# Experts of a two-layer trunk: TensorE's instructions in a written order, returns and gather beside the transposes, one pool of five banks

## The chip, the cores and the metric

The kernel runs on one core of a Trainium2 chip. The metric is the device time of one execution in microseconds. A smaller number is better. Engines are named as in the profile: PE is TensorE (PEld its weight loads), DVE is VectorE, ACT is ScalarE, POOL is GpSimd, and SP issues nearly all DMAs. PSUM, into which TensorE writes, has eight banks of 128 partitions x 512 fp32 values here; all eight are used by the experts.

## The reference

The whole program is a trunk of two layers over 256 latent and 256 context tokens of width 1024: modulation, three mixing branches (attention, a diagonal scan, a gated linear recurrence), and a mixture of experts. The change touches only the experts. Layer 0 sends context and latents through them, layer 1 the latents alone:

```python
def hier_moe(h, w_group, b_group, w_expert, b_expert, w_gate, w_up, w_down):
    ...
    top_p, top_i = lax.top_k(jax.nn.softmax(le_sel, axis=-1), TOP_K)
    wts = p_g[:, None] * top_p / jnp.sum(top_p, axis=-1, keepdims=True)
    ...
    def expert_block(args):
        xblk, e = args
        return (jax.nn.silu(xblk @ w_gate[e]) * (xblk @ w_up[e])) @ w_down[e]

    yb = lax.map(expert_block, (xb, blk_e)).reshape(cap, dm)
    out = jnp.zeros((n_tok + 1, dm), h.dtype).at[buf_tok].add(yb * buf_w[:, None].astype(h.dtype))
    return out[:n_tok]
...
            ctx = ctx_mid + g2c * hier_moe(hcf.reshape(-1, dm), *moe_par).reshape(ctx_mid.shape)
...
        x = x + g2 * hier_moe(hxf.reshape(-1, dm), *moe_par).reshape(x.shape)
```

There are 32 experts in a layer, each with `w_gate` and `w_up` of 1024 x 512 and `w_down` of 512 x 1024, in fp32.

## The kernel before

**Blocks.** Every expert gets 32 rows (`ROWS`) of each token set for the tokens that chose it; more would go through `overflow`, a loop that runs zero times on this data. One call of `expert_rows` works on a block of 128 rows. In layer 0 that is 2 experts x 2 sets (context and latents) x 32 rows, and there are 16 such blocks (`ng`). In layer 1 it is 4 experts x 32 rows, in 8 blocks.

**Steps of a block**, all in `expert_rows` but the gather:

- *gate* (tile `pg`) and *up* (`pu`): 32 matmuls each, with 32 columns of stationary data and 512 of moving data; four of them, one for each 32 rows of the block, use different columns of the array and stand next to each other in the code (the loop over `a`). Every fp32 matmul has two records in the trace.
- `hd`: silu by ACT, the product by DVE; then four *transposes* into `pt` and a copy by ACT to `hT` (also a tile `hd`).
- *down* (`py`, line 1689): two halves of 512 columns, 16 matmuls each, in groups of four as above. ACT scales a half to `wh`, DVE takes the remainder to `wl` (lines 1692 and 1695). `wh` and `wl` have one buffer each.
- *returns* (`pc`, line 1706): `wh` and `wl` of a half are spread back to tokens through the one-hot matrix `ot`: in layer 0 eight matmuls for a half, two (`wh`, `wl`) for each of four banks; the matmuls of the two token sets use different halves of the array's rows and stand in pairs in the code. DVE multiplies a bank by the gain (`cw`, line 1711, two buffers), POOL adds it to the residual (`Xctx`, `Xx`, line 1713).
- *gather* (`expert_gather`, tile `py`, line 1617): picks the next blocks' rows from `mh` by a one-hot matrix `oh`; in layer 0 one gather serves two blocks, with four banks of eight matmuls, and each bank is read out by four instructions, ACT and DVE in turn (lines 1629 and 1627, into `xT`). `expert_slots` (tile `pt`, line 1642) finds each row's weight and token with four short matmuls a block, read by DVE (`sl`).

**Banks.** `pg`, `pu` and `pt` have one bank each, pool `py` three (down and gather), pool `pc` two (returns).

**Order.** The program is written block after block: gate, up, transposes, down with its returns, then the next gather. The order on each engine is made by the framework's scheduler, which orders by its own timeline; each engine then runs its instructions in that order. The last block is written under a high priority.

**Weights.** `expert_chunk` takes weights as chunks of 128 x 2048 fp32 (1.05 MB), 12 for a block of layer 0 and 24 in layer 1, 192 in a layer. `prefetch` issues them on SP's queue (line 189) in the order of use, into a ring of 15 buffers in layer 0 (7 + 4 + 4) and 19 in layer 1 (11 + 4 + 4). A chunk can be issued when the matmuls that read the chunk 15 (19) places before it are done.

Of the kernel before, what the change touches and what calls it, by code (L numbers as in the profile page):

```python
# [18 lines left out]
NT = 4  # L19
# [107 lines left out]
class Trunk:  # L127
# [1409 lines left out]
    def moe(self, l, rs):  # L1537
# [8 lines left out]
        self.py = es.enter_context(tc.tile_pool(name=f"py{l}", bufs=3, space=PSUM))  # L1546
        self.pc = es.enter_context(tc.tile_pool(name=f"pc{l}", bufs=2, space=PSUM))
# [30 lines left out]
        def gather(q, OH):  # L1578

            w = na * ROWS  # L1580
            x = self.expert_gather(OH, nq)
            return [(x[:, :, a], self.expert_slots([OH[:, :, w * a:w * a + w]] * self.ns, m * q + na * a, aux)) for a in range(nq)]
# [6 lines left out]
        for _ in range(NXT[l] - PRE[l]):  # L1589
            self.prefetch(self.X[x0])  # L1590
        for p in range(ng):
            if p % nq == 0:
                cur = nxt
            W = [[self.expert_chunk() for a in range(na)] for _ in range(6)]
            if p < ng - 1:
                self.expert_rows(*cur[p % nq], na, self.ns, W)
            else:
                with tc.high_priority():
                    self.expert_rows(*cur[p % nq], na, self.ns, W, True)
            if p % nq == 0 and p + nq < ng:  # L1600
                nxt = gather(p // nq + 1, picked(p // nq + 1))
# [3 lines left out]
    def expert_gather(self, OH, nq, aff=None):  # L1605

        nc = self.nc
        nt = NT - self.mx0
        ns = 1 if aff else self.ns
        nt //= ns  # L1610
        xT = self.m2.tile([128, 8, nq, 128], FT, name="xT", bufs=2)
        for jj in range(0, 8, 4 // ns):
            xp = self.py.tile([128, 2, 256], FT, name="py").rearrange("p a (b n) -> p (a b) n", b=2)
            for u in range(4):
                j, s = jj + u // ns, u % ns
                for t in range(nt):
                    nc.tensor.matmul(xp[:, u, :], self.mh[:, nt * s + t, 128 * j:128 * j + 128], OH[:, nt * s + t, :],  # L1617
                                     start=t == 0 and u == 0, stop=t == nt - 1 and u == 3)
# [11 lines left out]
        return xT  # L1630

    def expert_slots(self, OHs, col, aux):

        nc = self.nc
        nt = NT - self.mx0
        ns, n = len(OHs), aux.shape[-1]
        nt //= ns
        w = 128 // ns
        ap = self.pg.tile([128, 512], FT, name="pt")
        for s, OH in enumerate(OHs):  # L1640
            for t in range(nt):
                nc.tensor.matmul(ap[w * s:w * s + w, 0:n], OH[:, nt * s + t, :], aux[:, nt * s + t, :], start=t == 0, stop=t == nt - 1)  # L1642
# [9 lines left out]
    def expert_rows(self, xT, sl, na, ns, W, last=False):  # L1652
# [10 lines left out]
        OT = self.ot  # L1663
        for t in range(nt // ns):
            V.tensor_scalar(OT[:, 128 * t:128 * t + 128], self.c["one1"], sl[:, 1:2], -128.0 * t, op0=OP.subtract, op1=OP.is_equal)
        P = []
        for n in range(2):
            q = pg.tile([128, 512], FT, name=f"p{'gu'[n]}")
            for hf in range(2):
                for k in range(4):  # L1670
                    for a in range(ng):
                        nc.tensor.matmul(q[ps_[a]], xT[:, 4 * hf + k, ps_[a]], part(W[2 * n + hf][a % na], k),  # L1672
# [4 lines left out]
        V.tensor_mul(hd, hd, P[1])  # L1677
        tp = pg.tile([128, 512], FT, name="pt").rearrange("p (j n) -> p j n", j=4)
        for j in range(4):
            nc.tensor.transpose(tp[:, j, :], hd[:, j * 128:(j + 1) * 128], self.ident)  # L1680
        hT = m2.tile([128, 512], FT, name="hd", bufs=1).rearrange("p (j n) -> p j n", j=4)
        S.copy(hT, tp)  # L1682
        for i, (c0, m) in enumerate(((0, 512), (512, 256), (768, 256)) if last else ((0, 512), (512, 512))):
# [3 lines left out]
            for k in range(4):  # L1687
                for a in range(ng):
                    nc.tensor.matmul(Y[ps_[a]], hT[:, k, ps_[a]], part(W[4 + n][a % na], k)[:, c1:c1 + m], start=k == 0, stop=k == 3)  # L1689
# [6 lines left out]
            cs = slice(c0, c0 + m)  # L1696
            nb = 512 // m
            nu = nt // ns
            for t in range(0, nu, nb):
                cps = [self.pc.tile([128, 512], FT, name="pc").rearrange("p (t n) -> p t n", t=nb) for _ in range(ns)]  # L1700
                for u in range(nb):
                    for y in (yh,) if whole else (yh, yl):
                        for s in range(ns):
                            r = slice(128 // ns * s, 128 // ns * (s + 1))
                            ot = OT[r, (t + u) * 128:(t + u + 1) * 128]
                            nc.tensor.matmul(cps[s][:, u], ot.bitcast(FT) if whole else ot, y[r],  # L1706
                                             start=(u == 0 if whole else y is yh), stop=(u == nb - 1 if whole else y is yl))
                for s in range(ns):
                    at = nu * s + t
                    w = m2.tile([128, 512], FT, name="cw").rearrange("p (t n) -> p t n", t=nb)  # L1710
                    V.tensor_mul(w, cps[s], self.g2[1 if x0 + at < 2 else 0][:, None, cs].to_broadcast([128, nb, m]))  # L1711
                    x = self.X2[(x0 + at) // 2 * 2][:, (x0 + at) % 2:(x0 + at) % 2 + nb, cs]
                    (V if nb > 1 and at + nb == nt else G).tensor_tensor(x, x, w, op=OP.add)  # L1713
            if last and nt == NT:
                for t in range(nt):
                    S.activation(cut(m2.tile([128, 512], FT, name="hd", bufs=1)), X[t][:, cs], AF.Square,
                                 accum_out=self.nsp[:, t, i:i + 1])

    def overflow(self, l, ov):
# [8 lines left out]
        with tc.If(n > 0), tc.For_i(0, n, 1) as i:  # L1728
# [54 lines left out]
            self.expert_rows(self.expert_gather(OH, 1, aff)[:, :, 0], sl, 1, 1, W)  # L1783
# [25 lines left out]
```

## Time and profile before

| | |
|---|---|
| median of 3 runs | 2107.39 us (2102.23 to 2111.22) |
| the profiled execution | 2102.93 us, span 2101.0 us |
| PE busy over the span | 1843.7 us (88%), 12480 records |
| DVE, ACT, POOL busy | 1036.6, 536.8, 503.2 us |
| HBM | 573.15 MB read, 292 GB/s over the span |
| granted TensorE clock, mean | 0.959 |

Times inside the execution are us from the start of the span. The stretches that matter: layer 0 before its experts up to 692, layer 0's experts from 692 to about 1243, the dense part of layer 1 to about 1640, layer 1's experts to the end. The rows below have the details. In the page's slices a digit stands for a fortieth of the span (52.5 us).

### The profile page before, as it was taken

The numbers are of one execution on the slowest core, as the hardware profiler recorded it, in microseconds if no ns is written. First come the engines' busy times: TensorE is split into PE (matmuls) and PEld (weight loads), VectorE is DVE, ScalarE is ACT, GpSimd is POOL, SyncE is SP. The second block draws the span as 40 slices with busy tenths as digits, with TensorE's granted clock in tenths as the row PEclk, the third lists the DMA queues.
The fourth block names the chain that finished last, engine by engine and source line by source line (L and its number), as shares of the span: only waits on it lengthen the run. The fifth ranks groups of instructions, "written<-read, shape, count | busy, mean of one in ns | idle before, by whom it ended". The sixth has DMA issues, their size and how long they took to land. (4 is left out here: it accounts for less than half of the span.)

```text
span 2101.0 us, 31835 instructions
## 1 busy us (share of the span) xinstructions
PE 1843.7 (88%) x12480; PEld 1113.4 (53%) x12480; DVE 1036.6 (49%) x2368; ACT 536.8 (26%) x1002; POOL 503.2 (24%) x473
## 2 busy tenths in 40 slices
PE   5889999999998999999999979989999776777776
PEld 2766776775787433433333239878888321222221
DVE  7858657979564233332333254958977310111111
ACT  3233533432333111110111034364444200000000
POOL 1632133405210032232313232215511000000000
PEclk8999999999998999999999989998999899999999
DMA  8576585557865798979888926646458999999998
GB/s 311 181 247 210 209 296 180 191 212 246 307 245 201 311 394 350 382 318 394 343 334 324 405 92 206 178 162 211 139 196 327 371 419 420 419 420 419 420 419 318
DMA packets 172048, 615.88 MB, mean 293 GB/s; under 512 B 24660, under 2 KB 90324, under 8 KB 108916
## 3 DMA queue, kind: packets, MB, share of 16 engines
q1 hardware_dynamic: 146084, 579.96, 71.6%
q10 hardware_dynamic: 25712, 33.56, 4.6%
q8 instruction: 100, 1.64, 0.3%
q14 instruction: 56, 0.46, 0.1%
q0 software_dynamic: 96, 0.26, 0.0%
HBM read 573.15 MB, written 40.58 MB: 292 GB/s over the span
## 5 line engine op out<-in xcount | busy, mean ns | idle before, releaser
L1672 PE MATMUL pg<-wst,xT 128*32 128x512 f32 x1536 | 252.7, 638 | 40.7 <-DMA wst<-mgate 38.6
L1672 PE MATMUL pu<-wst,xT 128*32 128x512 f32 x1536 | 233.1, 619 | 49.3 <-DMA wst<-mup 49.3
L367 DVE TENSOR_TENSOR wl<-wst,wh 128x512 fp32r<-128x512 f32 x240 | 192.9, 806 | 112.4 <-ACT wh L364 109.2
L1689 PE MATMUL py<-wst,hd 128*32 128x512 f32 (+1 forms) x1600 | 221.3, 578 | 21.7 <-ACT hd L1682 12.1
L364 ACT CAST wh<-wst 128x512 fp32r<-128x512 f32 x256 | 156.8, 618 | 281.3 <-PE acc L349 101.1
L1713 POOL TENSOR_TENSOR Xx<-Xx,cw 128x512 f32<-128x512 f32 x92 | 117.4, 1282 | 459.8 <-DVE cw L1711 459.8
L1677 DVE TENSOR_TENSOR hd<-hd,pu 128x512 f32<-128x512 f32 x24 | 16.5, 688 | 370.9 <-PE pu L1672 370.8
L1713 POOL TENSOR_TENSOR Xctx<-Xctx,cw 128x512 f32<-128x512 f32 x64 | 81.8, 1278 | 474.0 <-DVE cw L1711 473.9
L1711 DVE TENSOR_TENSOR cw<-pc,g 128x512 f32<-128x512 f32 x160 | 106.5, 687 | 152.2 <-PE pc L1706 148.0
L349 PE MATMUL acc<-hTh,wl 128*128 128x512 f32 (+1 forms) x480 | 168.1, 355 | 7.3 <-DVE wl L367 7.2
L347 PE MATMUL acc<-hTh,wh 128*128 128x512 f32 (+1 forms) x480 | 170.8, 356 | 1.3 <-ACT wh L364 1.3
L347 PE MATMUL acc<-wh,hTh 128*128 128x256 f32 x528 | 160.8, 309 | 11.5 <-ACT hTh L341 6.4
L348 PE MATMUL acc<-wl,hTh 128*128 128x256 f32 x528 | 161.2, 306 | 9.9 <-DVE wl L367 9.9
L348 PE MATMUL acc<-hTl,wh 128*128 128x512 f32 (+1 forms) x480 | 169.4, 353 | 0.0
L1672 PEld LDWEIGHTS pu<-wst,xT 128*32 128x32 f32 x1536 | 58.1, 113 | 196.9 <-issue 110.5
L349 PE MATMUL acc<-wh,hTl 128*128 128x256 f32 x528 | 160.1, 309 | 0.0
L1672 PEld LDWEIGHTS pg<-wst,xT 128*32 128x32 f32 x1536 | 55.7, 115 | 185.8 <-issue 112.5
L1689 PEld LDWEIGHTS py<-wst,hd 128*32 128x32 f32 x1600 | 58.7, 109 | 136.3 <-issue 91.6
L347 PEld LDWEIGHTS acc<-wh,hTh 128*128 128x128 f32 x528 | 112.2, 214 | 19.5 <-ACT hTh L341 7.0
L348 PEld LDWEIGHTS acc<-wl,hTh 128*128 128x128 f32 x528 | 113.5, 215 | 12.6 <-DVE wl L367 11.2
L1617 PEld LDWEIGHTS py<-oh,mh 128*128 128x128 f32 x768 | 96.2, 201 | 34.4 <-issue 29.6
L349 PEld LDWEIGHTS acc<-wh,hTl 128*128 128x128 f32 x528 | 111.9, 215 | 4.3 <-issue 3.0
(484 smaller groups left out, 3197.4 us busy)
## 6 DMA issues: line engine op xcount, KB each, us to landing
wst<-mgate SPq DMA_DIRECT2D x128, 1024.0 KB
wst<-mup SPq DMA_DIRECT2D x128, 1024.0 KB
wst<-mdown SPq DMA_DIRECT2D x122, 1024.0 KB
wst<-ada_w SPq DMA_DIRECT2D x48, 1024.0 KB
wst<-w_in SPq DMA_DIRECT2D x48, 1024.0 KB
wst<-w_o SPq DMA_DIRECT2D x8, 1024.0 KB
wst<-w_out SPq DMA_DIRECT2D x8, 1024.0 KB
dg<-stg ACTq DMA_DIRECT2D x15, 512.0 KB
```

The source lines that it names most:

```text
L347: nc.tensor.matmul(out, a[0], b[0], start=start, stop=False)
L348: nc.tensor.matmul(out, a[0], b[1], start=False, stop=False)
L349: nc.tensor.matmul(out, a[1], b[0], start=False, stop=stop)
L364: nc.scalar.copy(r(wh), s)
L367: e.tensor_sub(r(wl), s, r(wh).bitcast(FT))
L1617: nc.tensor.matmul(xp[:, u, :], self.mh[:, nt * s + t, 128 * j:128 * j + 128], OH[:, nt * s + t, :], start=t == 0 and u == 0, stop=t == nt ...
L1672: nc.tensor.matmul(q[ps_[a]], xT[:, 4 * hf + k, ps_[a]], part(W[2 * n + hf][a % na], k), start=hf == 0 and k == 0, stop=hf == 1 and k == 3)
L1677: V.tensor_mul(hd, hd, P[1])
L1689: nc.tensor.matmul(Y[ps_[a]], hT[:, k, ps_[a]], part(W[4 + n][a % na], k)[:, c1:c1 + m], start=k == 0, stop=k == 3)
L1711: V.tensor_mul(w, cps[s], self.g2[1 if x0 + at < 2 else 0][:, None, cs].to_broadcast([128, nb, m]))
L1713: (V if nb > 1 and at + nb == nt else G).tensor_tensor(x, x, w, op=OP.add)
```

## The change

`moe` makes one pool `py` of five banks in place of `py` (3) and `pc` (2). `self.pe` issues every matmul of a block behind the one before it in program order (`issue_after`), so that the scheduler no longer orders TensorE among the experts' matmuls; the other engines are still ordered by it. The returns of a half become a function, `expert_back`, which `expert_rows` hands back instead of running it; the next block runs the first half's returns between its up and its transposes (`before`), and behind its transposes the gather for a later block and the second half's returns (`behind`). A gather is cut in parts, so that each of the two blocks of layer 0 that share one runs half of it. The writes to `ot` move behind the returns that still read the old one. In the last block the first half's returns stand behind the second `down` piece.

```diff
-        self.py = es.enter_context(tc.tile_pool(name=f"py{l}", bufs=3, space=PSUM))
-        self.pc = es.enter_context(tc.tile_pool(name=f"pc{l}", bufs=2, space=PSUM))
+        self.py = es.enter_context(tc.tile_pool(name=f"py{l}", bufs=5, space=PSUM))
+        self.ordered, self.pe_last = False, None
...
+        back = ()
         for p in range(ng):
             if p % nq == 0:
                 cur = nxt
+                if p + nq < ng:
+                    OH = picked(p // nq + 1)
             W = [[self.expert_chunk() for a in range(na)] for _ in range(6)]
...
+            b = list(back)
+
+            def before():
+                if b:
+                    b.pop(0)()
+
+            def behind():
+                nonlocal nxt
+                if p // nq * nq + nq < ng:
+                    nxt = gather(p // nq + 1, OH, p % nq)
+                while b:
+                    b.pop(0)()
+            last = p == ng - 1
+            with self.in_order(), tc.high_priority() if last else nullcontext():
+                back = self.expert_rows(*cur[p % nq], na, self.ns, W, last, before, behind)
+                for f in back if last else ():
+                    f()
...
+    def pe(self, fn, *args, **kw):
+        if not self.ordered:
+            return fn(*args, **kw)
+        with nullcontext() if self.pe_last is None else self.tc.issue_after(self.pe_last):
+            i = fn(*args, **kw)
+        self.pe_last = i.ins
...
         V.tensor_mul(hd, hd, P[1])
+        before()
         tp = pg.tile([128, 512], FT, name="pt").rearrange("p (j n) -> p j n", j=4)
         for j in range(4):
-            nc.tensor.transpose(tp[:, j, :], hd[:, j * 128:(j + 1) * 128], self.ident)
+            self.pe(nc.tensor.transpose, tp[:, j, :], hd[:, j * 128:(j + 1) * 128], self.ident)
         hT = m2.tile([128, 512], FT, name="hd", bufs=1).rearrange("p (j n) -> p j n", j=4)
         S.copy(hT, tp)
+        behind()
+        OT = self.ot
+        for t in range(nt // ns):
+            V.tensor_scalar(OT[:, 128 * t:128 * t + 128], self.c["one1"], sl[:, 1:2], -128.0 * t, op0=OP.subtract, op1=OP.is_equal)
+        back = []
...
+            back.append(lambda c0=c0, m=m, yh=yh, yl=None if whole else yl, i=i: self.expert_back(c0, m, yh, yl, ns, last, i))
+            if not later or last and i:
+                back.pop(0)()
+        return back
...
+            cps = [self.py.tile([128, 2, 256], FT, name="py").rearrange("p a n -> p (a n)").rearrange("p (t n) -> p t n", t=nb) for _ in range(ns)]
```

TensorE in the middle of layer 0's experts before, from the transposes of a block on (the row of x4 at line 1680 is the transposes, `pg`/`pu`/`py<-wst` are gate, up and down, `pc` the returns; rows without a count are single matmuls):

```order
L1680 MATMUL pt<-cst_all,hd 128x128 x4
L1689 MATMUL py<-wst,hd 32x512 x17
L1706 MATMUL pc<-wh,ot 128x512 x2
L1689 MATMUL py<-wst,hd 32x512 x15
L1706 MATMUL pc<-wl,ot 128x512 x2
L1672 MATMUL pg<-wst,xT 32x512
L1706 MATMUL pc<-wh,ot 128x512
L1706 MATMUL pc<-wl,ot 128x512
L1706 MATMUL pc<-wh,ot 128x512
L1706 MATMUL pc<-wl,ot 128x512
L1672 MATMUL pg<-wst,xT 32x512 x15
```

The same engine and place now, a whole block (`py<-wh` and `py<-wl` are the returns, `py<-oh` the gather, `pt<-aux` the slots):

```order
L1635 MATMUL pg<-wst,xT 32x512 x32
L1635 MATMUL pu<-wst,xT 32x512 x32
L1635 MATMUL py<-wh,ot 128x512 x2
L1635 MATMUL py<-wl,ot 128x512 x2
L1635 MATMUL py<-wh,ot 128x512 x2
L1635 MATMUL py<-wl,ot 128x512 x2
L1635 MATMUL pt<-cst_all,hd 128x128 x4
L1635 MATMUL py<-oh,mh 128x128 x16
L1635 MATMUL pt<-aux,oh 64x33 x4
L1635 MATMUL py<-wh,ot 128x512 x2
L1635 MATMUL py<-wl,ot 128x512 x2
```

Two more returns rows and the 32 matmuls of down end the block, and the next begins. Gate, up and down are each in one piece, and the returns are in pairs throughout.

DVE in layer 0 before, from the product `hd` of one block to that of the next (`cw` are the returns' read-outs, two buffers that POOL empties; the next block in turn has the gather's):

```order
L1677 TENSOR_TENSOR hd<-hd,pu 128x512
L1695 SCALAR_TENSOR_TENSOR wl<-py,sl,wh 128x512
L1711 TENSOR_TENSOR cw<-pc,g_1_6567 128x512
L1711 TENSOR_TENSOR cw<-pc,g_0_6565 128x512
L1711 TENSOR_TENSOR cw<-pc,g_1_6567 128x512
L1695 SCALAR_TENSOR_TENSOR wl<-py,sl,wh 128x512
```

DVE now, the first part of a block, after the product `hd`:

```order
L1761 TENSOR_TENSOR cw<-py,g_1_6564 128x512
L1761 TENSOR_TENSOR cw<-py,g_0_6562 128x512
L1732 SCALAR_TENSOR_TENSOR wl<-py,sl,wh 128x512
L1761 TENSOR_TENSOR cw<-py,g_1_6564 128x512
L1761 TENSOR_TENSOR cw<-py,g_0_6562 128x512
L1659 TENSOR_SCALAR xT<-py,r_c_5800,mod_103 128x2x64 x2
```

The second half's `wl` stands between the first half's read-outs. What follows on DVE in a block whose gather part is the second of a gather (in the other blocks the row of `oh` is missing):

```order
L1679 COPY sl<-pt 32x1 x4
L1659 TENSOR_SCALAR xT<-py,r_c_5800,mod_103 128x2x64
L1680 COPY sl<-pt 128x1
L1568 TENSOR_TENSOR oh<-cst_moe,code_6457 128x128 x4
L1761 TENSOR_TENSOR cw<-py,g_1_6564 128x512
L1761 TENSOR_TENSOR cw<-py,g_0_6562 128x512
L1718 TENSOR_SCALAR ot<-cst_moe,sl 128x128
L1659 TENSOR_SCALAR xT<-py,r_c_5800,mod_103 128x2x64
```

The last read-out of the gather's second bank (`xT`, last row) stands behind two read-outs of the returns, a write of `ot` and, in every second block, four of `oh`.

## Rows read from the trace of the kernel before

**Rows 1.** The page's second part: GB/s moved by DMA in 40 slices.

```profile
GB/s 311 181 247 210 209 296 180 191 212 246 307 245 201 311 394 350 382 318 394 343 334 324 405 92 206 178 162 211 139 196 327 371 419 420 419 420 419 420 419 318
```

**Rows 2.** Busy time by stretch: PE, PEld, DVE, ACT, POOL, then clock, DMA share, GB/s.

```profile
1000.00:1060.00 60.00, 56.85 (x424) 18.27 (x423) 18.60 (x40) 6.72 (x12) 15.42 (x13) 1.00 0.88 352
1980.00:2040.00 60.00, 44.20 (x232) 14.07 (x228) 7.48 (x18) 4.39 (x8) 4.99 (x4) 0.89 1.01 420
```

**Rows 3.** Chain of work that ended last: start, us, what.

```profile
1667.17 19.90 DMA wst<-mgate
...
2089.59 3.64 PE py L1689 x52
```

**Rows 4.** PE's timeline, layer 0's experts: start, us, instructions [idle before <-releaser]; whole cycle.

```profile
692.22 8.65 PE L1672 MATMUL pg<-wst,xT 128*32 128x512 f32 x64 [2.13 <-ACTq L1728]
...
1022.32 0.66 PE L1680 MATMUL pt<-cst_all,hd 128*128 128x128 f32 x4 [0.85 <-DVE hd L1677]
1023.65 4.48 PE L1689 MATMUL py<-wst,hd 128*32 128x512 f32 x34 [0.68 <-ACT hd L1682]
...
1094.55 0.66 PE L1680 MATMUL pt<-cst_all,hd 128*128 128x128 f32 x4 [0.85 <-DVE hd L1677]
...
1237.03 0.51 PE L1706 MATMUL pc<-wh,ot 64*128 64x512 f32 x2
```

**Rows 5.** PE's timeline, two places where blocks of one kind stand whole.

```profile
700.68 7.05 PE L1672 MATMUL pu<-wst,xT 128*32 128x512 f32 x64
707.55 4.47 PE L1672 MATMUL pg<-wst,xT 128*32 128x512 f32 x36
...
774.20 7.07 PE L1689 MATMUL py<-wst,hd 128*32 128x512 f32 x64
781.20 0.49 PE L1617 MATMUL py<-oh,mh 128*128 128x128 f32 x2
```

**Rows 6.** PE's timeline, a mixed stretch of layer 0.

```profile
986.59 0.43 PE L1642 MATMUL pt<-aux,oh 128*64 128x33 f32 x8
986.95 1.04 PE L1689 MATMUL py<-wst,hd 128*32 128x512 f32 x2
987.93 2.05 PE L1617 MATMUL py<-oh,mh 128*128 128x128 f32 x16
989.91 0.51 PE L1706 MATMUL pc<-wh,ot 64*128 64x512 f32 x2
990.25 0.40 PE L1706 MATMUL pc<-wl,ot 64*128 64x512 f32 x2
990.57 1.38 PE L1617 MATMUL py<-oh,mh 128*128 128x128 f32 x10
```

**Rows 7.** Groups by form, 690 to 1250: busy us, mean ns | idle before <-releasers.

```profile
L1711 DVE TENSOR_TENSOR cw<-pc,g 128x512 f32<-128x512 f32 x128 | 85.2, 687 | 133.2 <-PE pc L1706 129.1 <-POOL Xctx L1713 4.1
L1713 POOL TENSOR_TENSOR Xctx<-Xctx,cw 128x512 f32<-128x512 f32 x64 | 81.8, 1278 | 474.0 <-DVE cw L1711 473.9
L1629 ACT ACTIVATE xT<-py,mod,r_c 128x128 f32<-128x128 f32 x58 | 26.3, 457 | 88.3 <-PE py L1617 60.5 <-DVE xT L1627 27.4
L1627 DVE TENSOR_SCALAR xT<-py,r_c,mod 128x128 f32<-128x128 f32 x59 | 24.0, 407 | 21.6 <-ACT xT L1629 21.3
L1695 DVE SCALAR_TENSOR_TENSOR wl<-py,sl,wh 128x512 fp32r<-128x512 f32 x31 | 23.1, 746 | 92.1 <-ACT wh L1692 92.1
L1665 DVE TENSOR_SCALAR ot<-cst_moe,sl 128x128 fp32r<-128x128 f32 x32 | 21.3, 670 | 0.0
L1692 ACT ACTIVATE wh<-py,sl 128x512 fp32r<-128x512 f32 x31 | 21.3, 688 | 164.2 <-PE py L1689 82.1 <-PE pc L1706 82.1
L1677 DVE TENSOR_TENSOR hd<-hd,pu 128x512 f32<-128x512 f32 x16 | 11.0, 688 | 109.7 <-PE pu L1672 109.6
L1648 DVE COPY sl<-pt 32x1 f32<-32x1 f32 x60 | 9.2, 153 | 18.7 <-PE pt L1642 18.1
L1568 DVE TENSOR_TENSOR oh<-cst_moe,code 128x128 f32<-128x128 f32 x28 | 8.6, 362 | 0.6 <-PE py L1617 0.6
```

More of the change, by code (lines that the diff above doesn't have):

```diff
@@ L1 @@
 import math
-from contextlib import ExitStack
+from contextlib import ExitStack, contextmanager, nullcontext
 import numpy as np
@@ L1577, in moe, with gather @@
         self.ot = self.m2.tile([128, nt * 128], FR, name="ot", bufs=1)
-        def gather(q, OH):
+        def gather(q, OH, part=None):
             w = na * ROWS
-            x = self.expert_gather(OH, nq)
-            return [(x[:, :, a], self.expert_slots([OH[:, :, w * a:w * a + w]] * self.ns, m * q + na * a, aux)) for a in range(nq)]
+            if not part:
+                self.gx, self.gs = self.m2.tile([128, 8, nq, 128], FT, name="xT", bufs=2), []
+            self.expert_gather(OH, self.gx, None if part is None else slice(2 * part, 2 * part + 2))
+            for a in range(nq) if part is None else (part,):
+                self.gs.append(self.expert_slots([OH[:, :, w * a:w * a + w]] * self.ns, m * q + na * a, aux))
+            return [(self.gx[:, :, a], s) for a, s in enumerate(self.gs)]
         if l == 0:
@@ L1593, in moe, with in_order, expert_gather @@
                 cur = nxt
+                if p + nq < ng:
+                    OH = picked(p // nq + 1)
             W = [[self.expert_chunk() for a in range(na)] for _ in range(6)]
[L1595 to L1601, printed above, removed]
+            b = list(back)
[13 more added lines that the diff above has]
+                    f()
         es.close()
         self.mes.close()
-    def expert_gather(self, OH, nq, aff=None):
+    @contextmanager
+    def in_order(self):
+        self.ordered = True
+        yield
+        self.ordered = False
+    def pe(self, fn, *args, **kw):
[4 more added lines that the diff above has]
+        self.pe_last = i.ins
+    def expert_gather(self, OH, xT, js=None, aff=None):
         nc = self.nc
@@ L1610, in expert_gather @@
         nt //= ns
-        xT = self.m2.tile([128, 8, nq, 128], FT, name="xT", bufs=2)
-        for jj in range(0, 8, 4 // ns):
+        for jj in range(0, 8, 4 // ns)[js or slice(None)]:
             xp = self.py.tile([128, 2, 256], FT, name="py").rearrange("p a (b n) -> p (a b) n", b=2)
@@ L1650, in expert_slots, with expert_rows @@
         return sl
-    def expert_rows(self, xT, sl, na, ns, W, last=False):
+    def expert_rows(self, xT, sl, na, ns, W, last=False, before=lambda: None, behind=lambda: None, later=True):
         nc = self.nc
@@ L1671, in expert_rows @@
                     for a in range(ng):
-                        nc.tensor.matmul(q[ps_[a]], xT[:, 4 * hf + k, ps_[a]], part(W[2 * n + hf][a % na], k),
+                        self.pe(nc.tensor.matmul, q[ps_[a]], xT[:, 4 * hf + k, ps_[a]], part(W[2 * n + hf][a % na], k),
                                          start=hf == 0 and k == 0, stop=hf == 1 and k == 3)
@@ L1688, in expert_rows @@
                 for a in range(ng):
-                    nc.tensor.matmul(Y[ps_[a]], hT[:, k, ps_[a]], part(W[4 + n][a % na], k)[:, c1:c1 + m], start=k == 0, stop=k == 3)
+                    self.pe(nc.tensor.matmul, Y[ps_[a]], hT[:, k, ps_[a]], part(W[4 + n][a % na], k)[:, c1:c1 + m], start=k == 0, stop=k == 3)
             whole = last and m < 512
@@ L1695, in expert_rows @@
                 V.scalar_tensor_tensor(yl, Y, sl[:, 0:1], yh.bitcast(FT), op0=OP.mult, op1=OP.subtract)
[L1696 to L1717, printed above, removed]
+            back.append(lambda c0=c0, m=m, yh=yh, yl=None if whole else yl, i=i: self.expert_back(c0, m, yh, yl, ns, last, i))
+            if not later or last and i:
+                back.pop(0)()
+        return back
+    def expert_back(self, c0, m, yh, yl, ns, last, i):
+        nc = self.nc
+        V, G, S = nc.vector, nc.gpsimd, nc.scalar
+        x0, m2, X, OT = self.mx0, self.m2, self.X, self.ot
+        nt = NT - x0
+        cut = lambda t: t[:, 0:m]
+        whole = yl is None
+        cs = slice(c0, c0 + m)
+        nb = 512 // m
+        nu = nt // ns
+        for t in range(0, nu, nb):
+            cps = [self.py.tile([128, 2, 256], FT, name="py").rearrange("p a n -> p (a n)").rearrange("p (t n) -> p t n", t=nb) for _ in range(ns)]
+            for u in range(nb):
+                for y in (yh,) if whole else (yh, yl):
+                    for s in range(ns):
+                        r = slice(128 // ns * s, 128 // ns * (s + 1))
+                        ot = OT[r, (t + u) * 128:(t + u + 1) * 128]
+                        self.pe(nc.tensor.matmul, cps[s][:, u], ot.bitcast(FT) if whole else ot, y[r],
+                                         start=(u == 0 if whole else y is yh), stop=(u == nb - 1 if whole else y is yl))
+            for s in range(ns):
+                at = nu * s + t
+                w = m2.tile([128, 512], FT, name="cw").rearrange("p (t n) -> p t n", t=nb)
+                V.tensor_mul(w, cps[s], self.g2[1 if x0 + at < 2 else 0][:, None, cs].to_broadcast([128, nb, m]))
+                x = self.X2[(x0 + at) // 2 * 2][:, (x0 + at) % 2:(x0 + at) % 2 + nb, cs]
+                (V if nb > 1 and at + nb == nt else G).tensor_tensor(x, x, w, op=OP.add)
+        if last and nt == NT:
+            for t in range(nt):
+                S.activation(cut(m2.tile([128, 512], FT, name="hd", bufs=1)), X[t][:, cs], AF.Square,
+                             accum_out=self.nsp[:, t, i:i + 1])
```

12 lines of the change are left out of this document (5 added, 7 removed).

## The prediction

> **What bounds the kernel now.** I read the slices first, to part the program into stages. In layer 1's experts, the last nine slices, DMA moves 419 GB/s without a break; in layer 0's experts, from slice 14 on, it moves 311 to 405 [rows 1]. The busy times by stretch say the same of a stretch of 60 us of each: layer 1 has a DMA share of 1.01 and PE 44.2 of 60 us, layer 0 has 0.88 and PE 56.9 [rows 2]. The chain that ended last is a line of DMA steps through layer 1, 19.90 us for the eight chunks of one gate [rows 3], so a chunk costs 2.49 us wherever DMA is the bound, and nothing that TensorE does there moves the end. The place to look is layer 0's experts, from 692.22 to the end of the last down at 1237.03, which is 544.8 us [rows 4].
>
> There a cycle of two blocks lasts 72.2 us, from the transposes at 1022.32 to those at 1094.55 [rows 4]. Its 24 chunks would take DMA 59.7. So TensorE's queue sets the pace. Yet its work is less: a whole gate, up or down takes 6.87 us (700.68 to 707.55, and 7.00 to an instruction of another kind, so 0.13 for the switch) [rows 5]; a gather bank 1.98, a block's slots 0.36, a pair of returns 0.34 or 0.32 [rows 6]; the transposes some 0.6 [rows 4]. A block is 3 x 6.87 + 2 x 1.98 + 0.36 + 16 returns in eight pairs, 2.7, + 0.6 = 28.2, two are 56.4. Waits for `hd` and `hT` are 2 x (0.85 + 0.68) = 3.1 [rows 4]. The other 12.7 us are the price of mixing: one matmul of down alone holds the engine for 0.98 us (986.95 to 987.93) [rows 6], where in a whole piece its share is 6.87 / 32 = 0.21. High busy time hides this.
>
> **The change, part by part: TensorE.** The new order has no broken groups and seven switches a block. With a gather a block is gate 6.87, up 7.00, returns 1.4, transposes 0.6, gather 3.95, slots 0.36, returns 1.4, down 6.87: 28.5 us. The wait for the product `hd`, 0.85, lies behind the first returns (1.4), and the copy to `hT` behind the gather; both cost nothing as long as these have their banks.
>
> **What is late next: banks.** The five banks of `py` turn in the order of their use, and a block takes twelve: four returns, two gather, four returns, two down. So the gather's first bank is the one that the second half of the previous down holds, and the first half of down takes the gather's second. The trace of before has no such turn, so I lay it out from its durations [rows 7], with 0 at the end of up and 0.05 for a signal.
>
> - `hd` is done at 0.85; PE has the first returns until 1.35 and the transposes until 1.95. DVE reads out two return banks until 2.25 (0.69 each). `wh` has one buffer, so ACT writes the second half's `wh` only when the first returns have read the old one, 1.2 to 1.9, and DVE its `wl` from 2.25 to 3.0. Only then is the bank free: the gather starts at 3.05, a **wait of 1.1**.
> - The gather runs to 6.95, the slots to 7.3, the second returns to 8.7. The other two `cw` wait for POOL, 1.28 an addition with two buffers, until 4.9, in time.
> - A bank of the gather is read by ACT, DVE, ACT, DVE, each waiting for the one before (27.4 and 21.3 us of idle time name each other [rows 7]), 0.46 and 0.41. For the second bank DVE has in its queue, from 7.4 on: four `sl` (0.6), `xT` to 8.45, one `sl`, two `cw` to 10.0, `ot` (0.67) to 10.65, and the last `xT` to 11.05. Down starts at 11.1 and could at 8.7: a **wait of 2.4**. In six blocks four `oh` stand there too, 4 x 0.36 = 1.45 more.
>
> So a block lasts 11.1 + 3 x 6.87 = 31.7. That is above DMA's 12 x 2.49 = 29.9, and the ring of 15 keeps ahead.
>
> **The sum.** First block, with no returns and a slower first gate (692.22 to 700.68): 8.46 + 7.05 + 0.85 + 0.6 + 3.95 + 0.36 + 6.87 = 28.1. Thirteen blocks of 31.7: 412.1. `oh` in six: 8.7. The last two have no gather; their second returns wait for `wl` until 3.05, and down for the fourth `cw` until 4.95, so 4.95 + 20.6 = 25.6 each, 51.1. In the last the first returns stand between the pieces of down: 1.4. Together 501.4, which is 43.4 less than 544.8.
>
> Layer 1's experts stay with DMA. Only the end is touched: the last chain step on PE [rows 3] holds both short pieces of down, and now four returns, 4 x 0.33, stand between them where before they fell into the waits for chunks: +1.3, bounds 0 and 1.5. The dense part of layer 1 has the same instructions, some in another place on PE, since the scheduler's timeline moved: 0, and as no row prices it I allow 6 either way. It waits on the experts' end, so the gain passes on.
>
> The profiled execution took 2102.9 (span 2101.0), so 2102.9 - 43.4 + 1.3 = 2060.8. The median of the runs is 4.5 above that execution; the range covers this.
>
> [...] Rows 5 price a switch between whole pieces at 0.13. [...]
>
> **Rivals.**
>
> *No bank waits, DMA sets the end.* If read-outs are quicker than laid out (`ot` is dearest, and only a mean), a block falls to 28.5, below DMA's 29.9. From the start 177 chunks are left to load, 441 us, and with the first and the last half piece, 3.4 each, the stage lasts some 450: 2009, or 2009 to 2040 where part of the waits goes. Against it: the one buffer of `wh` and `wl` and DVE's order are facts of the program.
>
> *The waits take all.* DVE and POOL are asked for the same work in bursts, `cw` behind POOL, `xT` behind `cw`. If the waits double, 3.5 more in 14 blocks or 49 us, the time is that of before, 2086 to 2112. For it: DVE waited for POOL already, 4.1 us [rows 7]; against it: POOL needs 8 x 1.28 = 10.2 of 31.7.
>
> *The clock.* In layer 1, where PE waits for every chunk, the granted clock falls to a mean of 0.89; in layer 0 it is 1.00 [rows 2]. If the new waits bring layer 0 to 0.89, each block's 28.5 us of work grow by 3.5, 56 in 16 blocks: 2117, slower than before. It decides from a loss of 2.7 a block, a mean clock below 0.91. Against it: two waits in 32 us, where layer 1 has one every 2.5, and the waits of 0.85 and 0.68 on both sides of the transposes left 1.00. [...]
>
> *TensorE was full.* If its 95% busy in layer 0 were all work, the order could bring nothing: 2103 to 2107. The 0.98 us for one matmul speaks against it, and the new order of the program does show whole pieces.
>
> **How the numbers follow.** The forecast, 2040 to 2086, has 0.67; no bank waits 0.15; waits that take all 0.10; the clock 0.06; TensorE full 0.02. One in ten lies below 2028 and one in ten above 2090: of the first rival a third is in the range, of the second little. A measurement of this kernel can tell about 0.5% from no change, 10.5 us. Faster by more: 0.67 + 0.15 + 0.05 of the second rival = 0.87; within: 0.07; slower: 0.06. The likeliest case gives 2061.
>
> **What would show it.** In the profile after: whole pieces of 6.87 us for gate, up and down in layer 0, and no single matmul of 0.98; a cycle of two blocks of some 64.9 instead of 72.2; PE idle for about 1.1 before the gather and 2.4 or 3.8 before down, with DVE as the releaser (`wl`, then `xT`); 380 to 400 GB/s; the stage some 43 us shorter; and layer 1's DMA steps still 19.9. Wrong would be: no idle before down, a granted clock under 1.00 in layer 0, or a dense part of layer 1 that differs by more than 6 us.

## The result, and the profile after

The changed kernel takes **2025.97 us** (median of 4 runs, 2022.45 to 2029.73) against 2106.44 of the kernel before (4 runs beside them, 2102.23 to 2111.22): ratio 0.9618, 95% interval 0.959 to 0.9645. The forecast was 2061 with a range of 2040 to 2086, and one chance in ten was put below 2028: the sign and the place were right, but the time lies under the range, and the gain was 80 us where 42 to 46 were expected. The profiled execution took 2025.23, span 2023.5.

DMA's line on the page, which answers to [rows 1]: slices 15 to 22 (counted from 1), layer 0's experts, now stand at 418 to 419 GB/s like layer 1's; before, the same slices stood at 318 to 394.

```profile
GB/s 323 164 236 257 142 353 193 171 167 255 239 365 113 251 418 418 419 418 419 418 419 418 359 103 244 131 201 191 102 250 366 419 420 419 420 420 419 420 420 293
```

Busy time by stretch (columns as in [rows 2]), first layer 0's experts in the kernel before, from the first gate to about the end of the last down:

```profile
692.22:1236.40 544.18, 526.72 (x3966) 195.75 (x3969) 169.04 (x353) 66.85 (x120) 151.44 (x121) 1.00 0.87 349
```

and the same stage in the kernel after, with the stretch of 60 us of [rows 2]:

```profile
694.19:1156.75 462.56, 441.90 (x3978) 186.05 (x3978) 171.01 (x357) 67.32 (x123) 152.05 (x122) 0.99 1.00 411
...
1000.00:1060.00 60.00, 57.43 (x525) 25.97 (x524) 24.15 (x51) 9.01 (x17) 22.13 (x18) 1.00 1.01 419
```

The stage is 82 us shorter, and PE's busy time fell by 85 with the same work; its idle time (first number less second) rose from 17.5 to 20.7. So the whole gain of the stage is time that the engine counted as busy and that was no work, and DMA's share went from 0.87 to 1.00.

PE's timeline of one block after, from its transposes to those of the next (columns as in [rows 4]):

```profile
968.81 0.66 PE L1635 MATMUL pt<-cst_all,hd 128*128 128x128 f32 x4
969.30 3.81 PE L1635 MATMUL py<-oh,mh 128*128 128x128 f32 x32
...
973.40 0.50 PE L1635 MATMUL py<-wh,ot 64*128 64x512 f32 x2
...
976.31 7.07 PE L1635 MATMUL py<-wst,hd 128*32 128x512 f32 x64 [1.69 <-DVE cw L1761]
983.20 7.05 PE L1635 MATMUL pg<-wst,xT 128*32 128x512 f32 x64
990.07 7.05 PE L1635 MATMUL pu<-wst,xT 128*32 128x512 f32 x64
997.05 0.50 PE L1635 MATMUL py<-wh,ot 64*128 64x512 f32 x2
...
998.17 0.66 PE L1635 MATMUL pt<-cst_all,hd 128*128 128x128 f32 x4
```

The pieces are whole, 6.87 us each; the block lasts 29.36, its neighbour (no `oh`) 28.55, the pair 57.9 us where 64.9 were forecast and DMA's 24 chunks take 59.7. There is no wait before the gather. The only wait left stands before down, 1.69 here and 0.87 in the neighbour, and its releaser is a read-out `cw`, not `xT`. DVE's timeline of the same block shows why this speaks against the prediction:

```profile
969.73 0.74 DVE L1732 SCALAR_TENSOR_TENSOR wl<-py,sl,wh 128x512 fp32r<-128x512 f32 x1
...
975.57 1.28 DVE L1761 TENSOR_TENSOR cw<-py,g 128x512 f32<-128x512 f32 x2
976.77 0.93 DVE L1718 TENSOR_SCALAR ot<-cst_moe,sl 128x128 fp32r<-128x128 f32 x1
977.62 0.40 DVE L1659 TENSOR_SCALAR xT<-py,r_c,mod 128x128 f32<-128x128 f32 x1
```

The gather began at 969.30, before `wl` had begun to read the bank of the last down half: it has another bank. Down began at 976.31, behind the first of the two `cw` at 975.57 and 1.3 us before the gather's last `xT`: it has a bank of the returns. The banks do not turn in the order of their use.

The end, which answers to [rows 3], in the chain after:

```profile
2000.31 8.59 DMA wst<-mdown
...
2008.95 7.56 PE py L1635 x66
```

From the last landing to the end of the span it is now 14.55 us, before 11.41.

### The profile page after: what moved, and what is told of

Its sections match the earlier page's. It is cut to its first block, busy times and chain, and to the rows that moved or that the text cites. A ratio compares the mean times of both kernels' runs of the same rounds, so it can differ in the third digit from the quotient of the medians.

```text
span 2023.5 us, 31822 instructions
## 1 busy us (share of the span) xinstructions
PE 1751.5 (87%) x12480; PEld 1102.0 (54%) x12480; DVE 1035.3 (51%) x2368; ACT 535.3 (26%) x1002; POOL 501.8 (25%) x473
## 5 line engine op out<-in xcount | busy, mean ns | idle before, releaser
L1635 PE MATMUL pu<-wst,xT 128*32 128x512 f32 x1536 | 220.6, 631 | 52.7 <-DMA wst<-mup 52.6
L1635 PE MATMUL pg<-wst,xT 128*32 128x512 f32 x1536 | 220.5, 640 | 49.5 <-DMA wst<-mgate 48.1
L1635 PE MATMUL py<-wst,hd 128*32 128x512 f32 (+1 forms) x1600 | 194.1, 594 | 41.7 <-DMA wst<-mdown 24.1
L347 PE MATMUL acc<-hTh,wh 128*128 128x512 f32 (+1 forms) x480 | 171.1, 357 | 1.5 <-ACT wh L364 1.5
L347 PE MATMUL acc<-wh,hTh 128*128 128x256 f32 x528 | 161.2, 310 | 10.6 <-ACT hTh L341 6.4
L1635 PEld LDWEIGHTS py<-wst,hd 128*32 128x32 f32 x1600 | 53.3, 113 | 169.0 <-issue 104.4
L1729 ACT ACTIVATE wh<-py,sl 128x512 fp32r<-128x512 f32 (+1 forms) x50 | 33.5, 670 | 369.2 <-PE py L1635 367.1
L347 PEld LDWEIGHTS acc<-wh,hTh 128*128 128x128 f32 x528 | 112.7, 216 | 17.0 <-ACT hTh L341 7.1
L1761 DVE TENSOR_TENSOR cw<-py,g 128x512 f32<-128x512 f32 x160 | 105.3, 685 | 27.1 <-PE py L1635 13.5
```

What stands on the lines that cost most here:

```text
L347: nc.tensor.matmul(out, a[0], b[0], start=start, stop=False)
L1635: i = fn(*args, **kw)
L1729: S.activation(yh, Y, AF.Identity, scale=sl[:, 0:1])
```

## The experiments

All times beside are of profiled executions. Every experiment but e8 and e10 was run once; single runs of the kernel before lie between 2094.8 and 2111.2, so a time that differs by less than some 10 us proves nothing by itself, and the timelines decide. "Stage" is from the first gate of layer 0's experts to the first matmul of the next dense part (L347 in the timelines); busy, idle and clock are of that stage without its last 21.5 us. What lies behind the last down is really 16.9 to 22.0 us in these runs, so busy time is up to 4.6 us too small (most in e5; 3.8 in e1 and e2); idle time is not touched by this. "Rounds" is counted from the order of PE's instructions, in layer 0's 16 blocks: in each stretch of weight matmuls between two instructions of another kind, the number of matmuls in the fullest of the four column tiles. With whole groups of four it is 384, and 6.87 / 8 = 0.86 us is one round.

| kernel | time | stage | PE busy | idle | clock | rounds |
|---|---|---|---|---|---|---|
| before | 2102.9 | 565.7 | 526.7 | 17.5 | 1.00 | 433 |
| after | 2025.2 | 484.1 | 441.9 | 20.7 | 0.99 | 384 |
| pool alone (e1) | 2057.8 | 514.8 | 465.7 | 27.6 | 1.00 | 402 |
| after, banks 3 + 2 (e2) | 2075.6 | 535.2 | 471.0 | 42.7 | 0.96 | 384 |
| after, order free (e3) | 2062.6 | 523.7 | 484.8 | 17.4 | 1.00 | 416 |
| after, banks in strict turn (e4) | 2073.6 | 534.8 | 457.4 | 55.9 | 0.96 | 384 |
| before's order, fixed (e5) | 2087.4 | 549.6 | 453.9 | 74.2 | 0.99 | 384 |
| returns in up, in groups (e6_mid) | 2076.2 | 533.1 | 464.7 | 46.9 | 0.99 | 399 |
| returns in up, between groups (e6_edge) | 2050.0 | 503.6 | 457.9 | 24.2 | 0.98 | 384 |
| returns in up, at steps (e9) | 2106.3 | 561.2 | 491.9 | 47.8 | 0.99 | 429 |
| half the returns (e7) | 2025.8 | 485.5 | 435.5 | 28.5 | 0.99 | 384 |

**Banks in strict turn** (e4). The step of the prediction in doubt, made true: five tiles of one buffer, taken by a counter.

```diff
+    def bank(self):
+        self.bn += 1
+        return self.py.tile([128, 2, 256], FT, name=f"py{'abcde'[self.bn % 5]}")
-            xp = self.py.tile([128, 2, 256], FT, name="py").rearrange("p a (b n) -> p (a b) n", b=2)
+            xp = self.bank().rearrange("p a (b n) -> p (a b) n", b=2)
```

(and so for `Y` and `cps`.) Expected:

> The changed kernel, in which the five banks for gather, returns and down are five tiles of one buffer each, taken in strict turn in the order of their use; all else is unchanged. Theory A (the prediction's reading of banks was right for a strict turn, and the changed kernel simply doesn't turn its banks): TensorE waits about 1.1 us before the gather for wl and 2.4 (3.8 with oh) before down for the last xT, two blocks take 63 to 66 us instead of 57.9, layer 0's experts some 500 us instead of 462.5, the time is about 2064. Theory B (the banks do turn, and my durations for the read-outs were too long): nothing changes, 57.9 and 462 us, 2026.

Its PE timeline, the two waits of a block and the one before down in its neighbour:

```profile
943.90 5.34 PE L1639 MATMUL pyd<-wst,hd 128*32 128x512 f32 x32 [3.36 <-issue]
949.02 3.64 PE L1639 MATMUL pye<-wst,hd 128*32 128x512 f32 x32
...
969.17 2.05 PE L1639 MATMUL pye<-oh,mh 128*128 128x128 f32 x16 [1.06 <-DVE wl L1736]
...
977.04 3.64 PE L1639 MATMUL pya<-wst,hd 128*32 128x512 f32 x32 [2.55 <-issue]
```

The layout of the prediction stands in it to a tenth: 1.06 before the gather (1.1), 2.55 before down (2.4), 3.36 with `oh` (3.85). The last `xT`, which down waits for there, reads `pya`, the bank that down then takes. The page puts down's wait to "issue", but DVE's timeline of this kernel has the last `xT` from 976.54 to 976.94, and down begins at 977.04. Even so the stage is 51 us longer than after's, not 38. By the table 35 of them are idle time and 15 busy time, and these are the clock: the first half of down at 943.90 takes 5.12 us where the second takes 3.44, and ten of the 16 blocks have such a slow first half (1.7 us longer each, one 2.7). The granted clock by stretch says so:

```profile
940.00:944.00 4.00, 0.64 (x10) 0.24 (x10) 3.97 (x12) 0.46 (x1) 1.87 (x2) 1.00 1.02 422
944.00:949.00 5.00, 5.00 (x32) 1.61 (x35) 1.91 (x3) 0.00 (x0) 3.14 (x3) 0.66 0.59 244
949.00:952.00 3.00, 3.00 (x32) 1.10 (x28) 0.75 (x1) 0.69 (x1) 0.00 (x0) 1.00 0.62 177
```

Theory A, with a part missing: the clock.

**Each half of the change alone** (e1 to e3). The pool alone, in the kernel before:

```diff
-        self.py = es.enter_context(tc.tile_pool(name=f"py{l}", bufs=3, space=PSUM))
-        self.pc = es.enter_context(tc.tile_pool(name=f"pc{l}", bufs=2, space=PSUM))
+        self.py = es.enter_context(tc.tile_pool(name=f"py{l}", bufs=5, space=PSUM))
```

(`cps` then comes from `py`.) Banks 3 + 2 is its mirror, the new order on the old pools:

```diff
-        self.py = es.enter_context(tc.tile_pool(name=f"py{l}", bufs=5, space=PSUM))
+        self.py = es.enter_context(tc.tile_pool(name=f"py{l}", bufs=3, space=PSUM))
+        self.pc = es.enter_context(tc.tile_pool(name=f"pc{l}", bufs=2, space=PSUM))
```

(`cps` comes from `pc` again.)

The free order is the kernel after with one line changed:

```diff
-        self.ordered = True
+        self.ordered = False
```

Expected:

> The kernel before with the one pool of five banks alone. Theory A (banks are not what it waits for, broken groups are): within 10 us of the kernel before, the stage 535 to 550 us. Theory B (the pool gives a good part of the gain): the stage at or below 520, 2080 or less.

> The changed kernel with the banks of before: three for gather and down, two for the returns. Theory A (the one pool is needed by the new order): the third and fourth bank of four returns wait for the read-outs of the first two, 1.5 us twice a block, so two blocks take 61 to 64 us in place of 57.9, the stage 480 to 500 in place of 462.5, the time 2043 to 2065. Theory B (the order alone matters): 57.9, 462.5, 2026.

> The changed kernel without the fixed order: the program's text stands as changed (returns and gather beside the transposes, one pool), but TensorE's instructions are placed by the scheduler's own estimate. It breaks about three groups of four in a block and puts the gather elsewhere than behind the transposes. Theory A (the fixed order carries the gain): a block costs 3 x 0.77 us for the broken groups and 1.5 for the waits for hd and hT more, two blocks take 64 to 66 us, the stage 510 to 525, the time 2075 to 2090. Theory B (the new places in the text carry it): 57.9 and 462.5 us, 2026.

My theory A for the pool fell: alone it shortens the stage by 51 us. In PE's timeline of that kernel the weights stand in far fewer stretches (63 in the stage; before 112, after 17), the returns in fours, and a broken group is left here and there:

```profile
954.72 0.66 PE L1679 MATMUL pt<-cst_all,hd 128*128 128x128 f32 x4 [0.90 <-DVE hd L1676]
956.05 1.05 PE L1688 MATMUL py<-wst,hd 128*32 128x512 f32 x2 [0.67 <-ACT hd L1681]
957.02 0.43 PE L1641 MATMUL pt<-aux,oh 128*64 128x33 f32 x8
957.39 3.63 PE L1688 MATMUL py<-wst,hd 128*32 128x512 f32 x30
...
1018.95 0.66 PE L1679 MATMUL pt<-cst_all,hd 128*128 128x128 f32 x4 [0.91 <-DVE hd L1676]
```

The cycle of two blocks is 64.2 (954.72 to 1018.95), before 72.2. The scheduler, with two banks for the returns, placed other work between single returns; with five it places them together. So part of the mixing came from the pools, which I had read only as a wait. The order alone (banks 3 + 2) gives 30 us, and its waits are the expected ones, for the read-outs of two banks:

```profile
PE pc L1636 <- DVE cw L1762: 39.0, 35, 2.2
```

Its time, 2075.6, lies above theory A's upper end (2065), again with a clock of 0.96. The free order keeps 42 of the 82 us: as theory A has it, the fixed order carries the other 40, though the total is better than its 2075. 51 and 30 add up to the whole, 82, though DMA may hold the whole down (e7 below).

**Whole pieces with nothing in the waits** (e5): the pool of five and the chain of the kernel after, on the text of the kernel before. The edit passes each matmul and transpose of the old functions through `pe`, and orders the whole loop over the blocks:

```diff
+        self.ordered = True
         for p in range(ng):
...
+        self.ordered = False
         es.close()
```

> The kernel before with one pool of five banks, and TensorE's order fixed to the order in which its program is written: each half of down is followed at once by its returns, the gather of a pair of blocks stands whole behind the first of them. So groups are unbroken, but nothing fills the waits for hd and hT, and the returns wait for wh and wl. Theory A (the broken groups are the price): two blocks take 56.4 of work + 1.8 of switches + 3.1 of waits for hd and hT + 5.2 of waits for wh and wl = 66.5 us in place of 72.2, the stage some 499 us in place of 544.8, 2057. Theory B (the gain comes from what was put into the waits, not from whole pieces): 72 us or more, 2103 or more.

The cycle is right, the time is not. PE's timeline, from transposes to transposes two blocks later, and some of the waits between:

```profile
975.39 0.66 PE L1611 MATMUL pt<-cst_all,hd 128*128 128x128 f32 x4 [0.91 <-DVE hd L1686]
976.72 3.64 PE L1611 MATMUL py<-wst,hd 128*32 128x512 f32 x32 [0.68 <-ACT hd L1691]
981.26 0.50 PE L1611 MATMUL py<-wh,ot 64*128 64x512 f32 x2 [0.89 <-ACT wh L1701]
...
1042.18 0.65 PE L1611 MATMUL pt<-cst_all,hd 128*128 128x128 f32 x4 [0.91 <-DVE hd L1686]
```

66.8 us, against 66.5 expected: 57.5 of work and 9.3 of waits. But I took the gain from one cycle of the kernel before, 72.2; its mean is 544.8 / 8 = 68.1, so the stage is only 16 us shorter. Whole pieces alone bring some 70 us of busy time and lose 57 of them as waits. With the returns and the gather set into these waits, the idle time falls from 74.2 to 20.7, some 54 us: where they stand is worth about as much as that they stand together.

**What a broken group costs** (e6, e9). In the kernel after, the four pairs of the first returns go into the up piece: `expert_back` becomes a generator that stops after each pair, and up's loop draws from it.

```diff
+                        if n and k % 2 and a == 0:
+                            next(mid, None)
```

In e6_edge it is `a == 3`, in e9 `a == (0, 1, 2, 0)[2 * hf + k // 2]`. Expected:

> The changed kernel, in layer 0 with the four pairs of the first returns set into the up piece between whole groups of four. Theory A (a change of kind between whole groups costs 0.13 us): six more changes make the block 0.8 us longer, and the wait for hd, 0.85, is no longer covered; two blocks take 60 to 62 us, the stage 465 to 480, the time 2030 to 2045. [...]

> The changed kernel, in layer 0 with the four pairs of the first returns set into the up piece, each pair behind the FIRST matmul of a group of four column tiles. Its pair is e6_edge, where each stands behind the fourth, between groups. Both lose the cover of the wait for hd, 0.85 us. Theory A (a broken group is dear): the up piece with its returns takes 4 x 0.77 = 3.1 us more than in e6_edge, two blocks 66 to 68 us in place of 60 to 62, the stage 515 to 535, the time 2080 to 2100. Theory B (every change of kind costs alike, broken or not): the same piece, the same cycle and time as e6_edge.

> As e6_mid, with the same number of returns in the up piece and each behind a broken group, but at steps: behind the first, the second, the third and the first matmul of a group, where e6_mid has all four behind the first. Theory A (the four column tiles are four queues of their own, each matmul of 512 columns holds its tile for 0.86 us, and a stretch of weights between two returns lasts as long as its fullest tile): the up piece needs 11 rounds of 0.86 us instead of 9 in e6_mid and 8 in e6_edge, so it takes 1.7 us longer than in e6_mid; 30 rounds in the stage, 26 us, the time about 2102. Theory B (a broken group has a price of its own, in e6_mid 0.25 us each, wherever it is broken): as e6_mid, 2076.

PE's timeline of up in e6_edge, from its first weights to the transposes behind:

```profile
946.50 1.90 PE L1639 MATMUL pu<-wst,xT 128*32 128x512 f32 x16
948.33 0.51 PE L1639 MATMUL py<-wh,ot 64*128 64x512 f32 x2
948.76 1.92 PE L1639 MATMUL pu<-wst,xT 128*32 128x512 f32 x16
...
956.16 0.66 PE L1639 MATMUL pt<-cst_all,hd 128*128 128x128 f32 x4 [0.48 <-DVE hd L1714]
```

Without the wait for `hd` the piece and its returns take 9.18 us, in the kernel after 8.10 (990.07 to 998.17): 1.08 for six more changes, **0.18 each**, near the 0.13 of [rows 5], so theory A, and far from the 0.33 that a change would cost if all 12.7 us of mixing in the cycle before went to its some 38 changes of kind (an estimate, 12.7 / 38, with the changes counted in PE's timeline from 1022.32 to 1094.55); the time lies 5 us above its range, with the wait for `hd` and a clock of 0.98. The same in e6_mid, where the first and the last stretch are broken groups:

```profile
955.84 1.88 PE L1639 MATMUL pu<-wst,xT 128*32 128x512 f32 x10
957.65 0.49 PE L1639 MATMUL py<-wh,ot 64*128 64x512 f32 x2
958.08 1.92 PE L1639 MATMUL pu<-wst,xT 128*32 128x512 f32 x16
...
964.94 1.06 PE L1639 MATMUL pu<-wst,xT 128*32 128x512 f32 x6
967.71 0.66 PE L1639 MATMUL pt<-cst_all,hd 128*128 128x128 f32 x4 [1.71 <-DVE hd L1714]
```

10.16 us, only 0.98 more for four broken groups. The rows tell why (a matmul is two instructions here): five matmuls take as long as eight, 1.81 and 1.85. Three left over from one group and one of the next fill the same round of the four tiles. What counts is the fullest tile, so four breaks in the same place cost one round. At steps they cost three, and in e9 the same stretches last a round longer:

```profile
937.09 1.88 PE L1639 MATMUL pu<-wst,xT 128*32 128x512 f32 x10
938.90 0.50 PE L1639 MATMUL py<-wh,ot 64*128 64x512 f32 x2
939.34 2.76 PE L1639 MATMUL pu<-wst,xT 128*32 128x512 f32 x18
...
950.62 0.66 PE L1639 MATMUL pt<-cst_all,hd 128*128 128x128 f32 x4 [1.71 <-DVE hd L1714]
```

11.82 us, 1.66 more than in e6_mid (two rounds are 1.72); the stage is 28 us longer (25.8 by rounds), the time 2106 (2102). Theory A holds. The time of e6_mid lay 4 us under its range, since it had expected a price for every break. In e6_mid and e9 the wait for `hd` is 1.71 and not 0.85, since DVE has the last read-outs of the returns and a `wl` in its queue ahead of it (965.11 to 966.98 in e6_mid): of the 29.5 us between the stages of e6_mid and e6_edge, some 18 are this wait (1.71 less 0.48 in 15 blocks), and some 13 are the one round (0.86 in 15 blocks).

**Half of the returns left out** (e7). The matmuls of `wl` in layer 0 are left out (`yl` is still made).

```diff
-                for y in (yh,) if whole else (yh, yl):
+                for y in (yh,) if whole or self.l == 0 and later else (yh, yl):
```

> The changed kernel without the low halves of layer 0's returns: the matmuls of wl, half of the returns, are left out, some 1.35 us of TensorE in each of 16 blocks, and nothing of DMA. Theory A (DMA now sets the end of the stage): TensorE waits for chunks instead, and the stage ends only as far earlier as the ring still has lead, at 450 us or more of the 462.5: 2014 to 2026. Theory B (TensorE still sets it): 16 x 1.35 = 21 us less, the stage 441, 2004.

PE's waits in that stage, and DMA's line of the page:

```profile
PE py L1635 <- DVE cw L1761: 18.7, 18, 1.2
PE pu L1635 <- DMA wst<-mup: 4.7, 6, 1.4
```

```profile
GB/s 323 180 233 248 157 340 193 168 172 254 254 372 110 250 418 419 419 418 419 418 419 419 336 112 238 128 195 197 97 258 368 415 420 420 419 420 419 420 419 292
```

PE is busy 6.5 us less, where 21 were expected, and idle 7.8 more: 3.3 of these are waits for chunks (4.7, in the kernel after 1.4), the rest nearly all waits for `hd` and `cw`. The stage is 485.5, 1.4 longer, so nothing was gained; theory B's 21 us were not put to the test. What speaks for theory A is the last block's up. In both kernels its second half waits for its chunk (first the kernel after, then e7):

```profile
1139.44 3.63 PE L1635 MATMUL pu<-wst,xT 128*32 128x512 f32 x30 [1.36 <-DMA wst<-mup]
```

```profile
1136.93 3.63 PE L1635 MATMUL pu<-wst,xT 128*32 128x512 f32 x30 [1.37 <-DMA wst<-mup]
```

From there TensorE has 17.4 us (18.7 in e7) to the end of down. So DMA sets when the stage can end in the changed kernel, and less work on PE ahead of that chunk gives nothing more. It is the only wait for a chunk in the stage of the kernel after, so there TensorE and DMA are nearly level.

**The end** (e8, with the kernel after again, e10). In the last block the first half's returns go ahead of the short pieces of down:

```diff
-            if not later or last and i:
+            if not later or last and i != 1:
```

> The changed kernel, where in the last block of a layer the returns of the first half stand before the first short piece of down and no longer between the short pieces. Theory A (the end was longer because these four returns came after the last chunk, and because TensorE did nothing in the wait for it, so that its clock was low behind it): from the last landing of down to the end 11.5 to 13.4 us in place of 14.55, the time 1 to 3 us shorter, 2023 to 2025. Theory B (the end has another cause): 14.5 us, 2026.

> The changed kernel as it is, beside e8_tail on the same chip, to see what a difference of one to three us in the end means: 2022 to 2030, 14.55 us from the last landing to the end, the start of layer 0's experts within 2 us of 694.

2023.69 (2018.92 to 2037.95, 4 runs) against 2026.83 for the kernel after again (2026.14 to 2034.37); against the kernel before 0.9638 (0.9587 to 0.9688) and 0.965 (0.9617 to 0.9683). Times cannot tell the two apart; the chains show the end, e8 first, then the kernel after again:

```profile
2000.38 8.73 DMA wst<-mdown
...
2009.15 6.23 PE py L1635 x62
```

```profile
2000.41 8.76 DMA wst<-mdown
...
2009.21 8.56 PE py L1635 x66
```

From the landing to the end it is 13.2 us in e8 and 15.5 and 14.55 in the two executions of the kernel after. The four returns are worth 1.1 of it (2012.37 to 2013.50 in the kernel after). The other half of theory A, the clock, was not taken away by this edit: behind the landing it is still 0.77 in e8 (2009 to 2016), as in the kernel after (0.77 and 0.59), and e8 too has waited 3.76 us for the last chunk with nothing to do. What it costs stands in the timeline of the kernel after, the weights ahead of the four returns and those behind them:

```profile
2008.95 3.49 PE L1635 MATMUL py<-wst,hd 128*32 128x256 f32 x26 [5.29 <-DMA wst<-mdown]
...
2013.50 1.93 PE L1635 MATMUL py<-wst,hd 128*32 128x256 f32 x32
```

The first 26 records take 3.42 us, at a granted clock of 0.53 (2008.95 to 2012.40), the 32 behind them 1.86, at 1.00 (2013.50 to 2015.40); both are eight in the fullest tile. In the kernel before the scheduler had spread returns over that wait, and the granted clock between 2084 and 2093.3 was 1.00.

## Why the prediction was right in sign and short by half

- **Bound by TensorE's order in layer 0, with DMA ready behind**: right. Busy time fell by 85 us, and 49 rounds of 0.86, 42 us, are broken groups; the other 43 go with fewer changes of kind (some 290 in the stage before, 93 after, with `wh` and `wl` as one kind; 0.18 each would be 35) and with returns of which the two row halves no longer stand apart. How these 43 divide was not tried.
- **The price of mixing**: the one lone matmul of 0.98 was read rightly, but such a row is one round with three idle tiles (in e6_mid five matmuls take 1.81 us and eight 1.85), not a price for every break. And 12.7 us is the price in one cycle of 72.2; over the stage the mean cycle is 68.1. The sum used neither, so this cost nothing.
- **Work of a block**: 28.5 forecast; 28.55 less its wait of 0.87 is 27.7, with 3.74 for the gather and 0.49 for the transposes.
- **Bank waits: the step that failed.** "The five banks of `py` turn in the order of their use" is not so. With a strict turn (e4) the waits are what was laid out; in the kernel after the one before the gather is missing, and the one before down is 0.87 or 1.69. PE's idle time in the stage is 20.7 where the laid out waits make 56 in e4. The stage was forecast at 501.4 and took 462.5 (694.19 to some 1156.7). Of the 501.4 some 58 are waits (0.85 in the first block, 3.5 in each of thirteen, 8.7 for `oh`, 1.6 in each of the last two), and 443 are work; the work measured is 441.9. So the miss of 39 us in the stage is in the waits. How the framework picks a bank for a tile was not tried; the runs show that it is not in strict turn.
- **So the rival "no bank waits, DMA sets the end", 0.15, is nearest to what happened**, though at 2026 and not 2009. Of the bank waits 17.0 us are left, nearly all before down, and two blocks with them still take less than DMA's 59.7. Its 441 us of transfers were about right, but it gave the ends 3.4 us each. DMA has its full rate only from some 701 on, 7 us into the stage, as the stretch here shows (20 us at 397 instead of 418), and behind the last chunk that TensorE waits for, at 1139.44, come 17.4 us of its work:

```profile
700.00:720.00 20.00, 19.10 (x181) 9.12 (x177) 3.26 (x11) 4.98 (x8) 0.00 (x0) 1.00 0.98 397
```

- **Waits that take all, TensorE full**: did not come. **The clock**: hardly in the kernel after (0.99, with one slow half of down, 5.06 us at 1118.01), but in e4 and e2, with 55.9 and 42.7 us of idle time, the stage stands at 0.96 (in e5, with 74.2, at 0.99), and the slow halves of down are some 15 us of e4's time.
- **A change of kind costs 0.18 us here** (e6_edge, 1.08 for six): a change has a price, and the runs do not show what the engine does in it. In e6_mid and e9 two groups share a round: five matmuls take 1.81 us, eight 1.85.
- **The end**: +3.1 where +1.3 was the term and 1.5 its upper bound. The four returns were right (1.1). Missing was the clock: 0.63 in the wait that they had filled (2004 to 2009) and 0.53 behind it (2008.95 to 2012.40), where it was 1.00 in the kernel before (2084 to 2093.3), and 3.42 us went on rounds that take 1.86 after the four returns.
- **Layer 1**: dense part 381.9 us, before 382.1, its experts' transfers within 0.8. The start of layer 0's experts came 2.0 later. So 2.0 - 81.6 - 0.2 - 0.8 + 3.1 = -77.5, the change of the span.

## What to carry to other kernels

Before you cost a wait for a buffer, find out from a trace of a kernel with such a pool whether its buffers really turn in strict order; if no trace shows it, both cases belong in the range, and the better one may end at the next bound. Count column-tiled matmuls in rounds of the fullest tile (here 0.86 us each, 433 in the stage before and 384 after) between two instructions of another kind: busy time that is more than the rounds is not work. A pool that is too small shows not only as a wait: a scheduler that knows of it scatters other work over the engine's queue, and that stands in the profile as busy time.

## What the runs showed of the hardware that was not expected

- A stretch of weights on the four 128 x 32 column tiles lasted as long as its fullest tile, 0.86 us (6.87 / 8) for each fp32 matmul of 512 columns, and a group broken in one place was completed together with the head of the next (five matmuls 1.81 us and eight 1.85 in e6_mid, nine at a shifted place 2.69 in e9: 939.34 to 942.03).
- A change between whole groups cost 0.18 us in e6_edge (0.13 in [rows 5]).
- Waits of 3.35 us before down in e4 were each followed by a slower stretch, 5.34 us for 16 matmuls instead of 3.64, so **1.70 us** each (at 744.98 2.7), with a granted clock of 0.66 behind the wait at 943.90 (944 to 949); of the waits of 2.55 some were followed by it (909.94, 1107.82) and some not (844.56, 977.04). Waits of 0.9 to 1.7 us in the kernel after left the clock at 1.00 from 700 to 1100, yet behind waits of only 0.49 a first half of down was slow at 1118.01 there (0.68 to 1123.10) and at 1166.64 and 1194.01 in e4. What decides between these is not settled by these runs.
